# The index keys' projection spread over the opening's four chunks of features, with one transfer per chunk for both weights, in a one-layer decoder kernel

## The chip, the core and the metric

The kernel runs on one core of a Trainium2 chip, as one program. A core has five engines with their own instruction queues: TensorE (PE in the profile) multiplies matrices into PSUM, VectorE (DVE) and ScalarE (ACT) do elementwise work and read PSUM, GpSimd (POOL) does small work and issues some transfers, and SyncE (SP) issues the others. The metric is the device time of one execution in microseconds, here 450.67 (median of three runs, 450.38 to 450.72).

## The reference

One layer of a decoder on 256 tokens of width 1024. The input is normalised, multiplied by one wide matrix, and split into three branches: block-sparse attention A, attention B whose keys are chosen by an indexer, and a recurrent branch C that starts with a causal convolution of `xc`. Cut to what this change is about:

```python
xn = rms_norm(x, g)
proj = xn @ w_in
(qa, ka, va, qb, kb, vb, qi, ki, wi, xc, yc, gates) = jnp.split(proj, IN_OFFSETS, axis=-1)
# indexer of branch B: 8 heads of qi (64 wide), one key ki (64 wide), 8 weights wi per token
dots  = jnp.einsum('bqhd,bsd->bqhs', qiq, ki)
score = jnp.einsum('bqh,bqhs->bqs', wq, jax.nn.relu(dots)) * idx_scale
# causal mask, top 64 keys of each token, attention over them
```

The columns of `w_in` in question: `qi` (512), `ki` and `wi` side by side (64 + 8 = 72, `KW` in the kernel), then `xc` (512) and `yc` (512). After the branches come sigmoid gates, an output projection, an MLP of width 4096 with squared ReLU, and a last normalisation.

## The kernel before, in words

**Precision.** Every f32 operand is split in two parts of a shorter format, `hi` (a copy on ScalarE, L134) and `lo` (the rest, a subtraction on VectorE, L135). A product is three passes: hi x hi, hi x lo, lo x hi (`PASSES`). So each weight tile of 128 x 1024 costs one ScalarE and one VectorE instruction before TensorE can use it, and both engines do this through the whole kernel.

**Weights.** They lie in DRAM as tiles in the order of use. `load` (L137) fetches tile `i` in two halves `raw{i}_0` and `raw{i}_1` of 128 x 1024 through SyncE's queue; five buffers hold raw halves, and a half's buffer is free when its `lo` has been made. `weights()` (L149) hands out the next tile; outside the part written by hand the Tile layer's scheduler places loads, splits and everything else by its own estimate of times.

**The opening** (L327 to L389) is placed by hand: inside `manual_schedule` the engines' instructions stand as written. The 1024 features come in four chunks of 256. For each chunk x (transposed, 256 KB) and a quarter of weight tile 0 (256 KB) are loaded (L232 to L235), ScalarE and VectorE split both, and TensorE makes 12 matmuls of the first half of the index queries, `ps_qi0` (L339 to L345): 2 feature tiles, 2 column tiles, 3 passes. Then follow the second half of the queries, `ps_qi1`, from tile 1; two matmuls that sum the squares of x over features into `ps_r` (L359); and the index keys and weights, `ps_kw`, 24 matmuls from a tile `kw` that is loaded and split as a whole (L238, L360, L376). Its 72 columns are padded with zeros to 128 by GpSimd (L275). In between VectorE computes 1/rms: the variance `v`, a power on GpSimd, one Newton step, `r1`, and two diagonal matrices `dg`, which TensorE multiplies by ones to spread r over all partitions (`rr`, L384). `first_queries(h)` (L284) takes the two halves of the queries out of PSUM. At the end (L386 to L389) the keys are scaled into `ki2`, `pair_keys` (L255) makes `keys2` on ScalarE and `keysl`, `keysh` on VectorE, and `wif` takes the index weights.

**Behind it** the scheduler places the projections `xc` (tiles 2 and 3, accumulators `ps_xc0`, `ps_xc1`), `yc` (tiles 4 and 5), then `vb`, `kb`, `qb` and so on, and puts the index logits (`l0_i0` and the following, L434), which need `keysh`, and the transposes of the index weights (`pt_wi`, L411), which need `wif`, between them. The accumulators share three PSUM buffers (`pacc`, L73): the next one waits until an earlier one has been taken out. `times` (L416) does that on VectorE for `xc`, `yc`, keys and queries. SyncE also reloads x in token order into the buffers of the transposed x (L563), after a small copy on GpSimd that needs `r1`.

Of the kernel before, what the change touches and what calls it, by code (L numbers as in the profile page):

```python
# [28 lines left out]
P = 128  # L29
# [30 lines left out]
def layer(ctx, tc, x, xf, wts, kiwi, small, wri, rel_bias, onehot, gfin, out):  # L60
# [16 lines left out]
    def f(ap):  # L77
        return ap.bitcast(F32)
# [7 lines left out]
    def big(name, dt=F32):  # L86
        return u4.tile([P, 1024], dt, tag="u4", name=name)
# [49 lines left out]
    def load(i):  # L137

        r = []
        for j in range(2):  # L140
            raw = wp.tile([P, 1024], F32, tag="raw", name=f"raw{i}_{j}", bufs=RAW_BUFS)
            nc.sync.dma_start(raw, wts[i, :, j * 1024:(j + 1) * 1024])
            r.append((raw, *(wp.tile([P, 1024], F32R, tag=p, name=f"{p}{i}_{j}", bufs=HL_BUFS) for p in ("hi", "lo"))))
        return r
# [68 lines left out]
    def tmajor(ps, w, xx, t, k0, nk, first, last):  # L213
# [3 lines left out]
        for n, (a, b) in enumerate(PASSES):  # L217
            for k in range(nk):
# [10 lines left out]
    w0 = [tuple(wp.tile([P, 1024], dt, tag=p, name=f"{p}0_{j}", bufs=n)  # L229
                for p, dt, n in (("raw", F32, RAW_BUFS), ("hi", F32R, HL_BUFS), ("lo", F32R, HL_BUFS)))  # L230
          for j in range(2)]
# [42 lines left out]
    for z in (kwh, kwl):  # L274
        nc.gpsimd.memset(f(z[:, :, KW:]), 0.0)  # L275
# [51 lines left out]
    with tc.manual_schedule(engines=ENGINES):  # L327
        pv = ps_q[0].rearrange("p (c t) -> p c t", c=2)
        for i in range(4):
            xi = xr[i // 2].rearrange("p (k t) -> p k t", k=4)  # L330
            d = slice(i % 2 * 512, (i % 2 + 1) * 512)
            raw, hi, lo = (z[:, d] for z in w0[i // 2])
# [6 lines left out]
            for n, (a, b) in enumerate(((0, 0), (0, 1), (1, 0))):  # L339
                for k in (2 * i, 2 * i + 1):  # L340
                    ww = w0[i // 2][1 + a].rearrange("p (k c) -> p k c", k=4)
# [18 lines left out]
        split(kwh[:, :, :KW], kwl[:, :, :KW], kw.rearrange("p (k c) -> p k c", c=KW))  # L360
        write_rows()

# [3 lines left out]
        first_queries(0)  # L366
# [22 lines left out]
        nc.vector.tensor_copy(wif[64:], ps_kw[64:, :S])  # L389
# [20 lines left out]
    for t in range(2):  # L410
        nc.tensor.transpose(pt[:, t * 64:(t + 1) * 64], wif[64:, t * P:(t + 1) * P], ident[64:, 64:])  # L411
    for t in range(2):
        nc.vector.tensor_scalar(wi[:, t, :], pt[:, t * 64:t * 64 + 8], r1[t], r1[t], op0=ALU.mult, op1=ALU.mult)
# [480 lines left out]
def _weight_tiles(w_in, w_pa, w_pb, w_pc, w_o, w_up, w_down):  # L894
# [14 lines left out]
    tiles.append(_fm(w_in[:, 3072:3328])), fm(w_in[:, 3328:3584])  # L909
# [20 lines left out]
    return np.ascontiguousarray(np.stack(tiles))  # L930

# [57 lines left out]
```

## Time and profile before

| | |
|---|---|
| Median of three runs | 450.67 us (450.38 to 450.72) |
| The profiled execution | 450.61 us, of which the traced span 448.8 us |
| TensorE busy | 440.0 us, 98% of the span, 2482 matmuls |
| VectorE busy | 349.6 us, 78% |
| ScalarE busy | 267.7 us, 60% |
| GpSimd busy | 24.1 us, 5% |
| Chain that ended last | TensorE 88%, transfers 4%, GpSimd 3%, VectorE 2% |
| Granted clock of TensorE | 0.999 of full speed on the mean |

How to read it: the page's first part gives busy time by engine, the fourth the chain of work that ended last. The list of waits says who stood still for whom. A timeline lists the instructions of an engine in order of time, equal ones that follow each other merged into one row with a count; the start is where the first of them starts, the duration of such a row reaches to the end of the last. Starts of successive rows give the pitch, which is what a queue of work costs; busy times of matmuls overlap. The names of tiles have their numbers left out in the trace: `ps_xc` is `ps_xc0` or `ps_xc1`, `lo<-raw,hi` any weight split.

### The profile page before, as it was taken

The numbers are of one execution on the slowest core, as the hardware profiler recorded it, in microseconds if no ns is written. First come the engines' busy times: TensorE is split into PE (matmuls) and PEld (weight loads), VectorE is DVE, ScalarE is ACT, GpSimd is POOL, SyncE is SP. The second block draws the span as 40 slices with busy tenths as digits, with TensorE's granted clock in tenths as the row PEclk, the third lists the DMA queues.
The fourth block names the chain that finished last, engine by engine and source line by source line (L and its number), as shares of the span: only waits on it lengthen the run. The fifth ranks groups of instructions, "written<-read, shape, count | busy, mean of one in ns | idle before, by whom it ended". The sixth has DMA issues, their size and how long they took to land.

```text
span 448.8 us, 6931 instructions
## 1 busy us (share of the span) xinstructions
PE 440.0 (98%) x2482; PEld 384.8 (86%) x2482; DVE 349.6 (78%) x687; ACT 267.7 (60%) x459; POOL 24.1 (5%) x61
## 2 busy tenths in 40 slices
PE   7999999999999999999999999999999999999994
PEld 7999899989988888888888888888888888888884
DVE  6799999999999999985888587666666666666646
ACT  6848496964467888675644466544444444444453
POOL 4820100000010100000000000000000000000000
PEclk9999999999999999999999999999999999999999
DMA  7998767436764462565555645465665566565202
GB/s 243 371 271 289 251 177 235 144 101 211 236 192 155 140 211 84 192 198 162 188 185 188 229 153 182 149 198 188 195 191 194 191 189 195 187 203 184 85 0 93
DMA packets 23838, 83.39 MB, mean 186 GB/s; under 512 B 2987, under 2 KB 3020, under 8 KB 23804
## 3 DMA queue, kind: packets, MB, share of 16 engines
q1 hardware_dynamic: 22608, 80.00, 54.6%
q0 software_dynamic: 960, 2.88, 2.3%
q8 instruction: 19, 0.31, 0.3%
q14 instruction: 15, 0.12, 0.1%
q10 hardware_dynamic: 236, 0.08, 0.1%
HBM read 81.11 MB, written 1.83 MB: 185 GB/s over the span
## 4 chain that ended last, share of the span: by engine, by line
PE 88%; DMA 4%; POOL 3%; DVE 2%; ACT 1%; issue 1%; SPq 0%; ACTq 0%; DVEq 0%; POOLq 0%
PE pd L815 19%; PE ps_g L219 15%; PE ps_up L209 13%; PE ps_p L219 7%; PE ps_up L211 7%; PE po L219 5%; DMA raw<-wts 3%; PE ps_qa L199 3%; PE ps_qb L199 3%; PE ps_kb L199 3%; PE ps_ka L199 3%; PE ps_va L219 2%; PE ps_vb L219 2%; DVE lo L135 1%; DMA x<-xf 1%
## 5 line engine op out<-in xcount | busy, mean ns | idle before, releaser
L135 DVE TENSOR_TENSOR lo<-raw,hi 128x1024 fp32r<-128x1024 f32 (+1 forms) x146 | 174.5, 1207 | 59.1 <-ACT hi L134 58.6
L134 ACT ACTIVATE hi<-raw 128x1024 fp32r<-128x1024 f32 (+1 forms) x146 | 149.8, 1045 | 93.1 <-issue 19.6
L209 PE MATMUL ps_up<-x,hi 128*128 128x512 f32 x256 | 64.7, 393 | 0.2 <-DVE x L186 0.2
L209 PEld LDWEIGHTS ps_up<-x,hi 128*128 128x128 f32 x256 | 46.7, 188 | 9.3 <-DVE x L186 0.4
L219 PE MATMUL ps_g<-hi,xn 128*128 128x512 f32 x192 | 53.7, 392 | 0.0
L815 PE MATMUL pd<-hi,hl 128*128 128x512 f32 (+1 forms) x128 | 49.5, 387 | 0.0
L815 PE MATMUL pd<-lo,hh 128*128 128x512 f32 (+1 forms) x128 | 49.4, 386 | 0.0
L815 PE MATMUL pd<-hi,hh 128*128 128x512 f32 (+1 forms) x128 | 49.1, 387 | 0.0
L219 PEld LDWEIGHTS ps_g<-hi,xn 128*128 128x128 f32 x192 | 35.6, 188 | 6.8
L211 PEld LDWEIGHTS ps_up<-x,lo 128*128 128x128 f32 x256 | 35.3, 190 | 2.7
L211 PE MATMUL ps_up<-x,lo 128*128 128x256 f32 x256 | 36.2, 282 | 0.0
L219 PE MATMUL ps_g<-lo,xn 128*128 128x512 f32 x96 | 30.2, 392 | 0.0
L815 PEld LDWEIGHTS pd<-lo,hh 128*128 128x128 f32 x128 | 24.0, 188 | 5.0
L815 PEld LDWEIGHTS pd<-hi,hh 128*128 128x128 f32 x128 | 24.0, 188 | 4.5
L815 PEld LDWEIGHTS pd<-hi,hl 128*128 128x128 f32 x128 | 24.1, 188 | 4.4
L802 ACT ACTIVATE hh<-z 128x512 fp32r<-128x512 f32 x16 | 10.1, 631 | 29.1 <-DVE z L800 29.1
L219 PEld LDWEIGHTS ps_g<-lo,xn 128*128 128x128 f32 x96 | 17.9, 188 | 3.6
L803 DVE TENSOR_TENSOR hl<-z,hh 128x512 fp32r<-128x512 f32 x16 | 11.1, 691 | 9.8 <-ACT hh L802 9.8
L168 POOL TENSOR_TENSOR ssq_n<-q_n 128x1 f32<-128x1 f32 x2 | 0.4, 192 | 277.6 <-ACT scr_n L166 277.6
L796 DVE TENSOR_TENSOR z<-ps_up,u 128x256 f32<-128x256 f32 x32 | 13.4, 418 | 0.0
L684 ACT ACTIVATE g<-ps_g,rh 128x512 f32<-128x512 f32 x12 | 8.2, 684 | 7.0 <-PE ps_g L219 7.0
L795 ACT ACTIVATE u<-ps_up 128x256 f32<-128x256 f32 x32 | 11.8, 368 | 0.0
(344 smaller groups left out, 777.1 us busy)
## 6 DMA issues: line engine op xcount, KB each, us to landing
raw<-wts SPq DMA_DIRECT2D x142, 512.0 KB, 4.8
x<-xf SPq DMA_DIRECT2D x4, 256.0 KB, 4.7
raw<-wts SPq DMA_DIRECT2D x4, 256.0 KB, 4.5
x<-x SPq DMA_DIRECT2D x2, 512.0 KB, 5.0
biasb<-toep POOLq DMA_DIRECT2D x8, 128.0 KB, 6.5
biasa<-toep POOLq DMA_DIRECT2D x8, 128.0 KB, 2.7
out<-o SPq DMA_DIRECT2D x2, 512.0 KB, 2.6
toep<-rrow POOLq DMA_DIRECT2D x1, 766.0 KB, 6.5
```

Of the source, the lines that this page charges most:

```text
L134: nc.scalar.activation(hi, raw, AF.Copy)
L135: nc.vector.tensor_sub(lo, raw, f(hi))
L199: nc.tensor.matmul(pv[:, c, :], ww[a][:, k, :], xx[b][:, k, :], start=(n == 0 and k == 0 and (c == 0 or not part)), stop=(n == 2 and k == ...
L209: nc.tensor.matmul(ps, wh[:, k, :], x2[:, k], start=(k == 0), stop=False)
L211: nc.tensor.matmul(ps[:, :S], wl[:, k, :], x2[:, k, 0], start=False, stop=(k == 7))
L219: nc.tensor.matmul(ps, xx[b][:, k0 + k, d], ww[a][:, k, :], start=(first and n == 0 and k == 0), stop=(last and n == 2 and k == nk - 1))
L684: nc.scalar.activation(g[:, t, :], ps, AF.Tanh, scale=rh[:, t:t + 1])
L795: nc.scalar.activation(u, ps[:, S:], AF.Copy)
L796: nc.vector.tensor_add(z[:, d], ps[:, :S], u)
L802: nc.scalar.activation(hh, z, AF.Copy)
L803: nc.vector.tensor_sub(hl, z, f(hh))
L815: nc.tensor.matmul(ps, hid[g][b][:, c, d], w_down[g][c][a][:, s], start=(g == (NG - LAG if o else 0) and c == 0 and m == 0), stop=(g == NG ...
```

## The change

Two things are moved. First, the index keys and weights: the kernel gets a new input `head`, four blocks of 128 x 656, in each the quarter of weight tile 0 that belongs to a chunk (512 columns) and the 144 columns of kw that belong to the same features; one transfer per chunk brings both. Each chunk splits its part of kw, and after its 12 matmuls of the queries come 6 of `ps_kw`, with 72 columns of weights loaded instead of 128. The separate load and split of `kw` and the zero padding go; `wif` and its transposes shrink to 8 columns. The four blocks take a raw buffer each; before, tile 0 took two.

Second, at the place where the 24 matmuls of `ps_kw` stood, the first half of `xc` (`cs=(0,)` of `ps_xc0`) now stands in the part placed by hand; `first_queries(0)` and the split of tile 2's first half are placed a few lines earlier. The scheduler places what follows anew.

```diff
+    w0r = [wp.tile([P, 1024], F32, tag="raw", name=f"raw0_{i}", bufs=RAW_BUFS)[:, :512 + 2 * KW] for i in range(4)]
     for i in range(4):
-        s, d = slice(i * 512, (i + 1) * 512), slice(i % 2 * 512, (i % 2 + 1) * 512)
-        nc.sync.dma_start(xr[i // 2][:, d], xf[:, s])
-        nc.sync.dma_start(w0[i // 2][0][:, d], wts[0, :, s])
+        nc.sync.dma_start(xr[i // 2][:, i % 2 * 512:(i % 2 + 1) * 512], xf[:, i * 512:(i + 1) * 512])
+        nc.sync.dma_start(w0r[i], head[i])
     loaded[1] = load(1)
-    kw = big("kw")[:, :8 * KW]
-    nc.sync.dma_start(kw, kiwi)
     loaded[2] = load(2)
...
-    for z in (kwh, kwl):
-        nc.gpsimd.memset(f(z[:, :, KW:]), 0.0)
...
             split(hi, lo, raw)
-            for n, (a, b) in enumerate(((0, 0), (0, 1), (1, 0))):
+            split(*(z[:, 2 * i:2 * i + 2, :KW] for z in (kwh, kwl)), kw)
+            for n, (a, b) in enumerate(PASSES):
...
+            for n, (a, b) in enumerate(PASSES):
+                for k in (2 * i, 2 * i + 1):
+                    nc.tensor.matmul(ps_kw[:KW, :S], (kwh, kwl)[a][:, k, :KW], xn[b][:, k, :],
+                                     start=(i == 0 and n == 0 and k == 0), stop=(i == 3 and n == 2 and k == 7))
...
-        split(kwh[:, :, :KW], kwl[:, :, :KW], kw.rearrange("p (k c) -> p k c", c=KW))
         write_rows()
+        first_queries(0)
 
         v, y, b = (sm.tile([P, 2], F32, name=f"{n}_n1", tag=n) for n in ("v", "y", "b"))
         nc.vector.tensor_scalar(v, ps_r[:, S:S + 2], 1.0 / DM, EPS, op0=ALU.mult, op1=ALU.add)
         nc.gpsimd.tensor_tensor(y, v, mhalf.to_broadcast([P, 2]), op=ALU.pow)
-        first_queries(0)
+        split_tile(2, 0)
...
-        split_tile(2, 0)
-        for n, (a, b) in enumerate(PASSES):
-            for k in range(8):
-                nc.tensor.matmul(ps_kw[:, :S], (kwh, kwl)[a][:, k, :], xn[b][:, k, :], start=(n == 0 and k == 0),
-                                 stop=(n == 2 and k == 7))
+        ps_xc = acc_tile("ps_xc0")
+        fmajor(ps_xc, [z[1:] for z in loaded[2]], xn, cs=(0,))
...
-        nc.vector.tensor_copy(wif[64:], ps_kw[64:, :S])
+        nc.vector.tensor_copy(wif[64:KW], ps_kw[64:KW, :S])
...
+        if h == 0:
+            ps = ps_xc
+            fmajor(ps, weights(), xn, cs=(1,))
...
+def _head(w, kw):
+    return np.stack([np.concatenate([_fm(z[i * 256:(i + 1) * 256]) for z in (w, kw)], axis=1) for i in range(4)])
```

What it does to the order of instructions shows at three places. In these rows a weight half keeps its tile's number: `lo4_1` is the lo part of the second half of tile 4. The last number of a name is only a counter, which differs between the two programs.

TensorE at the end of the opening, before: the second half of the queries, the sums of squares, the 24 matmuls of the keys, then xc.

```order
L199 MATMUL ps_qi1_165<-xn2_122,lo1_1_144 128x256 x8
L359 MATMUL ps_r_183<-ones_155,sqs_182 128x1 x2
L378 MATMUL ps_kw_166<-xn2_122,kwh_170 128x256 x16
L378 MATMUL ps_kw_166<-xn2_122,kwl_171 128x256 x8
L199 MATMUL ps_xc0_596<-xn2_122,hi2_0_149 128x256 x16
```

Here the 24 matmuls stand between the sums of squares and xc.

TensorE at the start of the opening now: the first chunk, and the start of the second.

```order
L340 MATMUL ps_qi0_164<-xn2_122,hi0_0_123 128x256 x8
L340 MATMUL ps_qi0_164<-xn2_122,lo0_0_124 128x256 x4
L345 MATMUL ps_kw_166<-xn2_122,kwh_170 72x256 x4
L345 MATMUL ps_kw_166<-xn2_122,kwl_171 72x256 x2
L340 MATMUL ps_qi0_164<-xn2_122,hi0_0_123 128x256 x8
```

The 24 matmuls of `ps_kw` stand in the chunks, six in each, and at their old place xc follows the sums of squares at once.

VectorE before, from the last split of tile 4's first half to the keys: the scaled keys `ki2`, the eviction of xc0 (`xp<-ps_xc0`), then `lo4_1`, the keys and `wif`.

```order
L135 TENSOR_TENSOR lo4_0_804<-raw4_0_801,hi4_0_803 128x1024
L387 TENSOR_TENSOR ki2_176<-ps_kw_166,rr_174 64x256 x2
L503 TENSOR_TENSOR wrl_591<-wrt_588,wrh_590 128x1024
L419 TENSOR_TENSOR xp_594<-ps_xc0_596,rr_174 128x2x256
L135 TENSOR_TENSOR lo4_1_808<-raw4_1_805,hi4_1_807 128x1024
L259 TENSOR_TENSOR keysl_159<-ki2_176,keys2_157 64x256
L260 CAST keysh_158<-keys2_157 64x128
L259 TENSOR_TENSOR keysl_159<-ki2_176,keys2_157 64x256
L260 CAST keysh_158<-keys2_157 64x128
L389 COPY wif_177<-ps_kw_166 64x256
L135 TENSOR_TENSOR lo5_0_876<-raw5_0_873,hi5_0_875 128x1024
L419 TENSOR_TENSOR xp_594<-ps_xc1_646,rr_174 128x2x256
```

The eviction of xc0 stands ahead of `lo4_1` here, and the keys ahead of `lo5_0`.

VectorE now, at the same place.

```order
L135 TENSOR_TENSOR lo4_0_808<-raw4_0_805,hi4_0_807 128x1024
L501 TENSOR_TENSOR wrl_620<-wrt_617,wrh_619 128x1024
L385 TENSOR_TENSOR ki2_174<-ps_kw_166,rr_172 64x256 x2
L135 TENSOR_TENSOR lo4_1_812<-raw4_1_809,hi4_1_811 128x1024
L417 TENSOR_TENSOR xp_623<-ps_xc0_388,rr_172 128x2x256
L135 TENSOR_TENSOR lo5_0_880<-raw5_0_877,hi5_0_879 128x1024
L417 TENSOR_TENSOR xp_623<-ps_xc1_650,rr_172 128x2x256
L256 TENSOR_TENSOR keysl_159<-ki2_174,keys2_157 64x256
L257 CAST keysh_158<-keys2_157 64x128
L256 TENSOR_TENSOR keysl_159<-ki2_174,keys2_157 64x256
L257 CAST keysh_158<-keys2_157 64x128
L387 COPY wif_175<-ps_kw_166 8x256
```

The split `lo4_1` stands ahead of the eviction of xc0, and `lo5_0` and the eviction of xc1 ahead of the keys and `wif`.

TensorE before, from the start of yc0 to the transposes of the index weights.

```order
L199 MATMUL ps_yc0_800<-xn2_122,hi4_0_803 128x256 x16
L199 MATMUL ps_yc0_800<-xn2_122,lo4_0_804 128x256 x8
L199 MATMUL ps_yc0_800<-xn2_122,hi4_1_807 128x256 x6
L434 MATMUL l0_i0_418<-keysh_158,qi_167 128x256
L434 MATMUL l0_i0_418<-keysl_159,qi_167 128x256
L434 MATMUL l0_i0_418<-keysh_158,qil_169 128x256
L411 MATMUL pt_wi_413<-ident_99,wif_177 128x64 x2
```

The logits cut into yc0 after 6 matmuls of its second half.

TensorE now, at the same place.

```order
L199 MATMUL ps_yc0_804<-xn2_122,hi4_0_807 128x256 x16
L199 MATMUL ps_yc0_804<-xn2_122,lo4_0_808 128x256 x8
L199 MATMUL ps_yc0_804<-xn2_122,hi4_1_811 128x256 x16
L199 MATMUL ps_yc0_804<-xn2_122,lo4_1_812 128x256 x2
L432 MATMUL l0_i0_447<-keysh_158,qi_167 128x256
L432 MATMUL l0_i0_447<-keysl_159,qi_167 128x256
L432 MATMUL l0_i0_447<-keysh_158,qil_169 128x256
L409 MATMUL pt_wi_442<-ident_99,wif_175 128x8 x2
```

The first index logits come 42 matmuls after the start of yc0, where they came after 30. In both programs the first matmul of yc0 waits for the eviction of xc0, whose buffer it takes.

## Rows read from the trace of the kernel before

**Rows 1.** Waits of TensorE, whole span: who waited for whom, us, times, longest.
```profile
PE ps_qi L343 <- ACT hi L134: 1.4, 1, 1.4
...
PE ps_up L209 <- DVE x L186: 0.2, 1, 0.2
```

**Rows 2.** Timeline of TensorE: start, us, what, count, [idle before and who ended it].
```profile
6.05 1.21 PE L343 MATMUL ps_qi<-xn,hi 128*128 128x256 f32 x8 [1.36 <-ACT hi L134]
...
7.82 1.22 PE L343 MATMUL ps_qi<-xn,hi 128*128 128x256 f32 x8
...
13.08 2.18 PE L199 MATMUL ps_qi<-xn,hi 128*128 128x256 f32 x16
...
19.66 0.50 PE L359 MATMUL ps_r<-ones,sqs 128*128 128x1 f32 x4
...
20.03 2.16 PE L378 MATMUL ps_kw<-xn,kwh 128*128 128x256 f32 x16
...
22.98 2.08 PE L199 MATMUL ps_xc<-xn,hi 128*128 128x256 f32 x16
```

**Rows 3.** Timeline of ScalarE, 0 to 30 us.
```profile
5.91 0.19 ACT L481 ACTIVATE sab<-sp 128x4 f32<-128x4 f32 x1
...
8.93 0.63 ACT L134 ACTIVATE hi<-raw 128x512 fp32r<-128x512 f32 x1 [0.32 <-DMA raw<-wts]
```

**Rows 4.** Timeline of VectorE, 20 to 39 us.
```profile
20.20 0.16 DVE L364 TENSOR_SCALAR v_n<-ps_r 128x2 f32<-128x2 f32 x1 [1.39 <-PE ps_r L359]
...
20.28 0.41 DVE L288 TENSOR_TENSOR qil<-ps_qi,qi 128x256 fp32r<-128x256 f32 x1
...
22.25 0.16 DVE L367 TENSOR_TENSOR b_n<-y_n 128x2 f32<-128x2 f32 x1 [0.19 <-POOL y_n L365]
...
23.45 1.21 DVE L135 TENSOR_TENSOR lo<-raw,hi 128x1024 fp32r<-128x1024 f32 x1
...
24.69 0.42 DVE L288 TENSOR_TENSOR qil<-ps_qi,qi 128x256 fp32r<-128x256 f32 x1
...
26.51 2.36 DVE L135 TENSOR_TENSOR lo<-raw,hi 128x1024 fp32r<-128x1024 f32 x2
...
31.30 0.86 DVE L387 TENSOR_TENSOR ki<-ps_kw,rr 64x256 f32<-64x256 f32 x2
...
33.33 0.69 DVE L419 TENSOR_TENSOR xp<-ps_xc,rr 128x512 f32<-128x512 f32 x1
...
33.93 1.22 DVE L135 TENSOR_TENSOR lo<-raw,hi 128x1024 fp32r<-128x1024 f32 x1
...
35.06 0.41 DVE L259 TENSOR_TENSOR keysl<-ki,keys 64x256 fp32r<-64x256 f32 x1
...
36.22 0.43 DVE L389 COPY wif<-ps_kw 64x256 f32<-64x256 f32 x1
...
37.67 1.23 DVE L135 TENSOR_TENSOR lo<-raw,hi 128x1024 fp32r<-128x1024 f32 x1 [1.02 <-ACT hi L134]
...
38.93 0.69 DVE L419 TENSOR_TENSOR xp<-ps_xc,rr 128x512 f32<-128x512 f32 x1
```

**Rows 5.** Timeline of TensorE, 34 to 39 us.
```profile
34.94 2.08 PE L199 MATMUL ps_yc<-xn,hi 128*128 128x256 f32 x16
...
38.54 0.28 PE L434 MATMUL l_i<-keysh,qi 128*128 128x256 f32 x1
...
38.99 0.34 PE L411 MATMUL pt_wi<-ident,wif 64*128 64x64 f32 x2
```

**Rows 6.** Timeline of ScalarE, near 36 us.
```profile
36.58 1.06 ACT L134 ACTIVATE hi<-raw 128x1024 fp32r<-128x1024 f32 x1 [2.13 <-DMA raw<-wts]
```

**Rows 7.** Chain that ended last, 0 to 80 us: start, us, what.
```profile
27.77 8.73 DMA raw<-wts
```

**Rows 8.** Timeline of VectorE, near 55 us.
```profile
54.73 0.69 DVE L419 TENSOR_TENSOR y<-ps_yc,rr 128x512 f32<-128x512 f32 x1
```

**Rows 9.** Timeline of TensorE, near 57 us.
```profile
56.85 1.09 PE L219 MATMUL ps_vb<-hi,xn 128*128 128x512 f32 x4
```

More of the change, by code (lines that the diff above doesn't have):

```diff
@@ L59, in layer @@
 @with_exitstack
-def layer(ctx, tc, x, xf, wts, kiwi, small, wri, rel_bias, onehot, gfin, out):
+def layer(ctx, tc, x, xf, head, wts, small, wri, rel_bias, onehot, gfin, out):
     nc = tc.nc
@@ L141, in load @@
             raw = wp.tile([P, 1024], F32, tag="raw", name=f"raw{i}_{j}", bufs=RAW_BUFS)
-            nc.sync.dma_start(raw, wts[i, :, j * 1024:(j + 1) * 1024])
+            nc.sync.dma_start(raw, wts[i - 1, :, j * 1024:(j + 1) * 1024])
             r.append((raw, *(wp.tile([P, 1024], F32R, tag=p, name=f"{p}{i}_{j}", bufs=HL_BUFS) for p in ("hi", "lo"))))
@@ L228, in layer @@
     xr = xt
-    w0 = [tuple(wp.tile([P, 1024], dt, tag=p, name=f"{p}0_{j}", bufs=n)
-                for p, dt, n in (("raw", F32, RAW_BUFS), ("hi", F32R, HL_BUFS), ("lo", F32R, HL_BUFS)))
+    w0 = [tuple(wp.tile([P, 1024], F32R, tag=p, name=f"{p}0_{j}", bufs=HL_BUFS) for p in ("hi", "lo"))
           for j in range(2)]
+    w0r = [wp.tile([P, 1024], F32, tag="raw", name=f"raw0_{i}", bufs=RAW_BUFS)[:, :512 + 2 * KW] for i in range(4)]
     for i in range(4):
-        s, d = slice(i * 512, (i + 1) * 512), slice(i % 2 * 512, (i % 2 + 1) * 512)
-        nc.sync.dma_start(xr[i // 2][:, d], xf[:, s])
-        nc.sync.dma_start(w0[i // 2][0][:, d], wts[0, :, s])
+        nc.sync.dma_start(xr[i // 2][:, i % 2 * 512:(i % 2 + 1) * 512], xf[:, i * 512:(i + 1) * 512])
+        nc.sync.dma_start(w0r[i], head[i])
     loaded[1] = load(1)
-    kw = big("kw")[:, :8 * KW]
-    nc.sync.dma_start(kw, kiwi)
     loaded[2] = load(2)
@@ L331, in layer @@
             d = slice(i % 2 * 512, (i % 2 + 1) * 512)
-            raw, hi, lo = (z[:, d] for z in w0[i // 2])
+            hi, lo = (z[:, d] for z in w0[i // 2])
+            raw, kw = w0r[i][:, :512], w0r[i][:, 512:].rearrange("p (k c) -> p k c", c=KW)
             for k in (2 * i, 2 * i + 1):
@@ L410, in layer @@
     for t in range(2):
-        nc.tensor.transpose(pt[:, t * 64:(t + 1) * 64], wif[64:, t * P:(t + 1) * P], ident[64:, 64:])
+        nc.tensor.transpose(pt[:, t * 8:(t + 1) * 8], wif[64:KW, t * P:(t + 1) * P], ident[64:KW, 64:KW])
     for t in range(2):
-        nc.vector.tensor_scalar(wi[:, t, :], pt[:, t * 64:t * 64 + 8], r1[t], r1[t], op0=ALU.mult, op1=ALU.mult)
+        nc.vector.tensor_scalar(wi[:, t, :], pt[:, t * 8:(t + 1) * 8], r1[t], r1[t], op0=ALU.mult, op1=ALU.mult)
     def times(dst, ps, row):
@@ L508, in layer @@
     for h in range(2):
-        ps = acc_tile(f"ps_xc{h}")
-        fmajor(ps, weights(), xn)
+        if h == 0:
+            ps = ps_xc
+            fmajor(ps, weights(), xn, cs=(1,))
+        else:
+            ps = acc_tile(f"ps_xc{h}")
+            fmajor(ps, weights(), xn)
         times(xp[:, 2 * h:2 * h + 2, 3:], ps, rr)
@@ L907, in col @@
         return w_in[:, o:o + 512]
-    tiles.append(_fm(w_in[:, 3072:3328])), fm(w_in[:, 3328:3584])
+    fm(w_in[:, 3328:3584])
     fm(col(3656)), fm(col(4168))
@@ L970 @@
         "xf": _fm(i["x"][0].T),
+        "head": _head(w_in[:, 3072:3328], w_in[:, 3584:3656]),
         "wts": _weight_tiles(w_in, i["w_pa"][0], i["w_pb"][0], i["w_pc"][0], i["w_o"][0],
                              i["w_up"][0], i["w_down"][0]),
-        "kiwi": _fm(w_in[:, 3584:3656]),
         "small": small,
```

2 lines of the change are left out of this document (1 added, 1 removed).

## The prediction

> **What bounds the kernel now.** I read the page's busy shares first: TensorE is busy for 98% of the span, so a change gains only where TensorE stands still, or by giving it less to do. The list of waits says where it stands still: by its first and its last row [rows 1] TensorE waits for data once at the start and 0.2 us much later, and nothing else of note. The timeline then shows the start in detail [rows 2]. The opening works through four chunks of features; twelve matmuls of the index queries take from 6.05 to 7.82 us, and all 48 end at 13.08, that is 7.03 us. Further on 30 matmuls of the same shape take from 34.94 to 38.54 [rows 5], 0.12 us each. So 48 cost 5.76 us and 1.27 us of the opening is idle, split over four chunks. That is all there is to win here. ScalarE sets the chunks' pace, and at the third its split of the raw weights waits for their transfer [rows 3].
>
> After 13.08 TensorE is dense to the end, so whatever moves its work at 13 us moves the end by the same, unless a new wait comes in between. Whether one does is read from VectorE, which works almost without a break from 20 us on [rows 4].
>
> **The opening, part by part.** The 24 matmuls of index keys and weights stand now at 20.03 to 22.98 [rows 2], 2.95 us. They move into the chunks, six to each. They stay 24 matmuls of 256 columns, so no work goes away; they fill the idle time. 72 matmuls at 0.12 are 8.64 us. I let the first start 0.1 later, since a small activation (0.19 us, [rows 3]) now stands ahead of the first split, and choose another 0.1 for a late second half of the first chunk. The opening then ends at 6.05 + 0.2 + 8.64 = 14.89.
>
> Can the chunks keep up? They come every 1.77 us now (7.82 - 6.05) and TensorE will need 18 x 0.12 = 2.16 per chunk. The weights of a chunk grow from 512 to 656 columns beside 512 of x, 14% more bytes, so a supply bound by transfers comes every 2.02 us; were all of it bound by the weights' transfer it would be 2.27, which costs 3 x 0.11 = 0.33 us. I take 0 and keep 0.33. The kw splits on ScalarE and VectorE, 144 columns per chunk, fit into the 0.39 us by which the period grows; the two fills of kwh and kwl leave GpSimd, which TensorE waits for nowhere in [rows 1].
>
> From 13.08 to the two sums of squares at 19.66 it is 6.58 us [rows 2], unchanged, so they start at 21.47 and the xc half placed by hand 0.37 later (20.03 - 19.66), at 21.84, against 22.98 now: 1.14 us ahead. From there to yc0, the next accumulator, TensorE has the same 48 + 48 matmuls as now, 34.94 - 22.98 = 11.96 us [rows 2, 5]. Without a wait yc0 would start at 33.80.
>
> **The new wait.** yc0 takes the PSUM buffer of xc0, so it waits until VectorE has scaled xc0 out of it. Now that eviction ends at 33.33 + 0.69 = 34.02 and yc0 starts at 34.94 [rows 4, 5]: 0.92 us to spare. In the new order VectorE has one full weight split more (lo4_1) ahead of this eviction, and its chain hangs on the sums of squares. By the pitches of [rows 4], from the start of those sums (19.66): 0.54 to the variance, 0.08 for it, 1.24 for lo2_0, 1.20 for the Newton steps and the two diagonals (22.25 to 23.45), 1.82 for the second queries (24.69 to 26.51), 4.79 for lo2_1 to lo4_0 (26.51 to 31.30), 2.03 for ki2 and wrl (31.30 to 33.33), 1.13 for lo4_1 (33.93 to 35.06), 0.69 for the eviction: 13.52 us. The first queries, which lie behind the variance now, move ahead of it into idle time (VectorE waits 1.39 us there). So xc0's buffer is free at 21.47 + 13.52 = 34.99. TensorE arrives at 33.80 and waits 1.19 us; yc0 starts 0.05 later than now, and the gain is gone. As both paths hang on the sums of squares, an opening that is 0.1 faster or slower moves this sum by 0.1 and no more. With 0.3 us of error in the chain the result here lies between -0.25 and +0.35.
>
> That wait exists because VectorE doesn't look past the split. The row shows the habit: at 37.67 VectorE starts a split after waiting 1.02 us for ScalarE, and the eviction of xc1 at 38.93 stands behind it, though TensorE had finished xc1 before yc0 began at 34.94 [rows 4, 5]. The Trainium skill says it as a rule (PSUM — Partial Sum Buffer, "Engine vs sequencer instructions"): the queues of ScalarE, VectorE and GpSimd are strictly first in, first out. It speaks against this change, and the trace agrees; were evictions able to pass, the sum would be 1.13 us lower.
>
> **The keys behind it.** After yc0 starts, 42 matmuls follow (24 of its first half, 18 of its second) before the first index logits, 5.04 us: TensorE is there at 40.03. These need keysh, and 0.45 us later (38.54 to 38.99, [rows 5]) the transposes need wif. Both now come behind lo5_0 and xc1's eviction on VectorE, and lo5_0 waits for hi5_0, which waits for its transfer. Now ScalarE gets it at 36.58 [rows 6], after a transfer that is issued when lo2_1 is done and takes 8.73 us [rows 7]. In the new order lo2_1 starts at 21.47 + 0.54 + 0.08 + 1.24 + 1.20 + 1.82 = 26.35, 0.16 earlier than its 26.51, so with the same transfer lo5_0 starts at 37.67 - 0.16 = 37.51. Then 1.26 to xc1's eviction, 0.60 for that (33.33 to 33.93), 1.16 for the keys (35.06 to 36.22): keysh is ready at 40.53, half a microsecond after TensorE asks; wif 0.43 later, which the 0.45 covers. If the transfer lands 0.5 us sooner this wait is 0. Ahead of it in the queue one weight tile now goes before the two x loads instead of behind them, the same bytes, so the row alone gives no sign; I take the middle, 0.25, and keep 0 and 0.5.
>
> VectorE falls behind by its longer stand at lo5_0: it could start it at 34.90 (0.60 after the eviction of xc0 starts) and does at 37.26 (the middle), 2.36 us instead of 1.02, less the 0.16, so about 1.2 us. Its eviction of yc0 at 54.73 [rows 8] then ends at 54.73 + 0.69 + 1.18 = 56.60, and the V projection that takes the buffer comes at 56.85 + 0.3 [rows 9]. That still fits by half a microsecond.
>
> The transposes of wi shrink from 64 to 8 columns: 0 to 0.34 us of gain, since the two take 0.34 in all [rows 5]; TensorE waits for their input anyway, and I take 0. Everything else is the same work in nearly the same order under a dense TensorE.
>
> **The sum.** +0.05 at yc0 and +0.25 at the keys: +0.3 us on the profiled execution, which took 450.61 in all. That makes 450.9; the median of the runs is 450.67, so the two stand 0.06 apart. A difference within 0.2%, 0.9 us, is what a measurement of this kernel cannot tell from none.
>
> **Rivals.** *The opening's gain is kept.* VectorE would have to reach xc0's eviction 1.13 us sooner than the pitches say, as if lo4_1 were not ahead of it. Then -1.14 + 0.05 gives 449.5. For it: VectorE has 1.39 us of idle time before the variance, which a shorter path to it would use. Against: the split stands there in the order, and each pitch is a row. Chance 0.07.
>
> *Narrow weights are cheaper.* The 24 moved matmuls load 72 columns of weights instead of 128. If their time went with the loaded columns, 2.95 x 56/128 = 1.29 us would go, the sums of squares would come that much sooner and VectorE's chain with them: 449.6. [Rows 2, 5] speak against: the matmuls run at 0.12 us back to back with 128 loaded columns, and what they stream, 256 columns, stays. Chance 0.04. The Trainium skill (TensorE: Matmul & The Clock Gate, "LDWEIGHTS (loading the stationary operand)") does state that a load's time goes with its columns; no run here shows a load of 72.
>
> *The keys come late: slower.* The mechanism is the transfer of raw5_0. It is issued behind two x loads that wait for r1, and the steps from the variance to r1 and the diagonals end about 1 us later than now (21.47 + 0.54 + 0.08 + 1.24 + 1.20 = 24.53 instead of 23.45, [rows 4]), so these loads sit closer ahead of it. If hi5_0 starts 1 us later than the row's 36.58 allows, at 37.42, keysh is ready at 41.53 and TensorE waits 1.5 us: 450.61 + 0.05 + 1.5 = 452.2. From 0.35 us of lateness the total is slower by more than 0.9. For it: the 8.73 us of [rows 7] show a queue that is long already. Against: the tile ahead of it is issued sooner than now. Chance 0.20.
>
> *The forecast,* a gain in the opening that a wait on VectorE takes back, has 0.69, with 450.4 to 451.5 as its own range: its ends are -0.25 and 0 at yc0 and the keys, and +0.35 + 0.5. The range of 449.7 to 451.9 takes in the near part of the others.
>
> **What would show it.** The opening's matmuls end near 14.9 without gaps, and the sums of squares start near 21.5. The timeline of TensorE has a gap of 1 us or more at yc0, ended by VectorE's eviction of xc0, and a smaller one at the first index logits, ended by keysh. VectorE's lo4_1 starts near 33.2, and lo5_0 waits over 1 us for ScalarE. The forecast is wrong if TensorE is dense from 14.9 to 40, or if the sums of squares come at 21 or sooner.

## The result, and the profile after

The changed kernel takes 455.44 us (455.07 to 456.62, 4 runs) where the kernel before took 450.70 beside it (450.38 to 451.49, 4 runs): a ratio of 1.0104, 95% interval 1.0086 to 1.0123. It is 1% slower, far outside the forecast range (449.7 to 451.9). The profiled execution took 455.36 us, its span 453.6 against 448.8.

TensorE's waits say at once that more than the forecast wait is there (who waited for whom, us, times, longest; [rows 1] had 1.4 and 0.2):

```profile
PE ps_qi L340 <- ACT hi L134: 2.2, 1, 2.2
PE ps_yc L199 <- DVE xp L417: 1.7, 1, 1.7
...
PE l_i L432 <- ACT rl L443: 0.8, 1, 0.8
PE l_i L432 <- DVE keysh L257: 0.5, 1, 0.5
...
```

TensorE's timeline puts them in order of time (start, us, what, count, idle before). It answers to [rows 2, 5]:

```profile
7.09 1.55 PE L340 MATMUL ps_qi<-xn,hi 128*128 128x256 f32 x8 [2.20 <-ACT hi L134]
8.45 1.05 PE L340 MATMUL ps_qi<-xn,lo 128*128 128x256 f32 x4
9.30 1.05 PE L345 MATMUL ps_kw<-xn,kwh 128*72 128x256 f32 x4
...
10.58 1.38 PE L340 MATMUL ps_qi<-xn,hi 128*128 128x256 f32 x8
...
16.58 0.64 PE L345 MATMUL ps_kw<-xn,kwh 128*72 128x256 f32 x4
17.06 0.40 PE L345 MATMUL ps_kw<-xn,kwl 128*72 128x256 f32 x2
17.30 2.08 PE L199 MATMUL ps_qi<-xn,hi 128*128 128x256 f32 x16
...
23.78 0.50 PE L360 MATMUL ps_r<-ones,sqs 128*128 128x1 f32 x4
24.14 2.16 PE L199 MATMUL ps_xc<-xn,hi 128*128 128x256 f32 x16
...
38.17 2.15 PE L199 MATMUL ps_yc<-xn,hi 128*128 128x256 f32 x16 [1.73 <-DVE xp L417]
...
43.90 0.39 PE L432 MATMUL l_i<-keysh,qi 128*128 128x256 f32 x1 [0.47 <-DVE keysh L257]
...
48.77 0.39 PE L432 MATMUL l_i<-keysh,qi 128*128 128x256 f32 x1 [0.85 <-ACT rl L443]
```

Read the starts. The first product begins at 7.09, not 6.05. The first chunk's 18 products take until 10.58, 3.49 us where 18 x 0.12 = 2.16 were forecast: four products need 0.85 us (8.45 to 9.30), 0.21 each. The last chunk is at full speed, narrow products too: four in 0.48 us (16.58 to 17.06). TensorE's granted clock says why (stretch, busy times, and as the third column from the end the granted clock, PEclk):

```profile
6.00:8.00 2.00, 0.91 (x6) 0.91 (x7) 1.81 (x5) 2.00 (x8) 0.00 (x0) 0.94 1.03 388
8.00:10.00 2.00, 2.00 (x12) 2.00 (x11) 2.00 (x7) 1.89 (x7) 1.21 (x3) 0.50 0.79 188
10.00:12.00 2.00, 2.00 (x14) 2.00 (x13) 1.36 (x4) 0.63 (x2) 1.74 (x6) 0.71 0.88 300
```

It falls to 0.50, the 1.2 GHz level, after TensorE had stood idle for 2.20 us; whether the idle time is the reason is tested below. ScalarE's timeline shows what the start waited for, and what the keys do later:

```profile
5.52 0.91 ACT L330 ACTIVATE xn<-x,sp 128x256 fp32r<-128x256 f32 x2 [2.85 <-DMA sp<-small]
...
39.87 1.06 ACT L134 ACTIVATE hi<-raw 128x1024 fp32r<-128x1024 f32 x1 [7.24 <-DMA raw<-wts]
40.84 1.71 ACT L255 ACTIVATE keys<-ki 64x256 fp32r<-64x256 f32 x4
...
46.46 1.99 ACT L134 ACTIVATE hi<-raw 128x1024 fp32r<-128x1024 f32 x2
48.35 0.84 ACT L443 ACTIVATE rl<-l_i 128x256 f32<-128x256 f32 x2
```

The table of small parameters, sp, lands 4.8 us after its issue; before it was 3.8. These are the rows of the transfers, after and before (KB, then us from issue to landing):

```profile
sp<-small ACTq DMA_DIRECT2D x1, 24.0 KB, 4.8
```

```profile
sp<-small ACTq DMA_DIRECT2D x1, 24.0 KB, 3.8
```

The split of a late weight tile, hi5_0, starts at 39.87 after ScalarE has waited 7.24 us for its transfer, and the copies of the keys stand behind it. That transfer is issued when lo2_1 is done, as forecast, and takes 9.16 us where [rows 7] had 8.73:

```profile
30.63 9.16 DMA raw<-wts
```

VectorE's chain behind the sums of squares is the forecast one, a little longer ([rows 4]):

```profile
24.32 0.16 DVE L365 TENSOR_SCALAR v_n<-ps_r 128x2 f32<-128x2 f32 x1 [0.40 <-PE ps_r L360]
24.51 1.23 DVE L135 TENSOR_TENSOR lo<-raw,hi 128x1024 fp32r<-128x1024 f32 x1
26.36 0.16 DVE L368 TENSOR_TENSOR b_n<-y_n 128x2 f32<-128x2 f32 x1 [0.62 <-POOL y_n L366]
...
29.38 2.36 DVE L135 TENSOR_TENSOR lo<-raw,hi 128x1024 fp32r<-128x1024 f32 x2
...
31.78 2.35 DVE L135 TENSOR_TENSOR lo<-raw,hi 128x1024 fp32r<-128x1024 f32 x2
34.05 1.22 DVE L501 TENSOR_TENSOR wrl<-wrt,wrh 128x1024 fp32r<-128x1024 f32 x1
35.30 0.87 DVE L385 TENSOR_TENSOR ki<-ps_kw,rr 64x256 f32<-64x256 f32 x2
36.20 1.23 DVE L135 TENSOR_TENSOR lo<-raw,hi 128x1024 fp32r<-128x1024 f32 x1
37.34 0.68 DVE L417 TENSOR_TENSOR xp<-ps_xc,rr 128x512 f32<-128x512 f32 x1
40.97 1.22 DVE L135 TENSOR_TENSOR lo<-raw,hi 128x1024 fp32r<-128x1024 f32 x1 [2.94 <-ACT hi L134]
42.11 0.68 DVE L417 TENSOR_TENSOR xp<-ps_xc,rr 128x512 f32<-128x512 f32 x1
42.71 0.41 DVE L256 TENSOR_TENSOR keysl<-ki,keys 64x256 fp32r<-64x256 f32 x1
```

At 26.36 VectorE waits for GpSimd's power. GpSimd's rows for it, after and before:

```profile
24.57 1.76 POOL L366 TENSOR_TENSOR y_n<-v_n,mhalf 128x2 f32<-128x2 f32 x1 [1.93 <-DVE v_n L365]
```

```profile
21.35 0.86 POOL L365 TENSOR_TENSOR y_n<-v_n,mhalf 128x2 f32<-128x2 f32 x1
```

Term by term:

| term | forecast | trace after |
|---|---|---|
| first product | 6.15 | 7.09 |
| opening, 72 products | 8.64 (and 0.1) | 10.21 (7.09 to 17.30) |
| sums of squares at | 21.47 | 23.78 |
| from there to the end of xc0's eviction | 13.52 | 14.24 (to 38.02) |
| wait at yc0 | 1.19 | 1.73 |
| wait at the first index logits | 0.25 | 0.47 |
| wait at the second | 0 | 0.85 |
| yc0 starts at, against 34.94 before | 34.99 | 38.17 |

So 3.23 us are lost by yc0, and 0.47 + 0.85 more at the logits: 4.55 of the span's 4.8.

### The profile page after: what moved, and what is told of

Same layout as the page of the kernel before. It is cut to its first block, busy times and chain, and to the rows that moved or that the text cites. A ratio compares the mean times of both kernels' runs of the same rounds, so it can differ in the third digit from the quotient of the medians.

```text
span 453.6 us, 6933 instructions
## 1 busy us (share of the span) xinstructions
PE 441.2 (97%) x2482; PEld 386.4 (85%) x2482; DVE 349.6 (77%) x690; ACT 267.4 (59%) x462; POOL 24.5 (5%) x59
## 4 chain that ended last, share of the span: by engine, by line
PE 92%; DMA 3%; ACT 3%; DVE 1%; issue 1%; ACTq 0%
PE pd L817 19%; PE ps_g L219 14%; PE ps_up L209 13%; PE ps_p L219 7%; PE ps_up L211 7%; PE po L219 5%; PE ps_qa L199 3%; PE ps_qb L199 3%; PE ps_ka L199 3%; PE ps_kb L199 3%; PE ps_vb L219 2%; PE ps_va L219 2%; DMA raw<-wts 2%; ACT hi L134 2%; PE ps_qi L340 2%; PE ps_qi L199 1%
```

## The experiments

Each ratio is to the kernel before, run beside it on the same chip. "Before" and "changed" in a line say from which kernel it was made.

### The first product's late start

**blocks_alone.** Changed, with the 24 products and the first xc group put back where the kernel before has them; only the loads and the splits by chunk stay.

> The changed loads alone: the four blocks of 656 columns and the splits of the keys' columns with their chunk, but the 24 products of the keys stand where the kernel before has them and the first group of xc is the scheduler's again. Theory D (the bigger blocks make the small table and the first chunk of x land later): the small table lands 4.8 us after its issue instead of 3.8, the first product starts at 7.1 instead of 6.05, and with 9 warming products the granted clock falls as well; time 452.0 to 453.0. Rival E (the late landing has to do with the rest of the change or is chance of one execution): first product near 6.05, clock 1.00, 450.4 to 451.0.

Measured: 452.57 us, ratio 1.0045 (1.0032 to 1.0057). sp lands after 4.6 us, first product at 6.90, granted clock 0.56 from 8 to 10 us. The loads alone cost 2.0 us by the ratio, before a single product has moved.

**rows_768, rows_apart, two_transfers.** Changed, with the rows padded, spaced, or fetched in two parts:

```
-  w0r = [wp.tile(...)[:, :512 + 2 * KW] for i in range(4)]
+  w0r = [wp.tile(...)[:, :768] for i in range(4)]       # rows_768; head padded with zeros
...
-  nc.sync.dma_start(w0r[i], head[i])
+  nc.sync.dma_start(w0r[i], head[:, i*656:(i+1)*656])  # rows_apart: blocks side by side
+  nc.sync.dma_start(w0r[i][:, :512], head[i, :, :512])   # two_transfers
+  nc.sync.dma_start(w0r[i][:, 512:], head[i, :, 512:])   # two_transfers
```

> The changed kernel with each block's rows filled with zeros from 656 to 768 columns (2,624 to 3,072 bytes), so the opening loads 0.23 MB more. Theory F (bytes on the queue ahead make the small table late): it lands later than 4.8 us after its issue, by as much again for 112 columns as for 144, so near 5.5; first product near 7.7, time 456 to 457. Rival G (the odd length of a row makes packets slow): it lands 3.8 us after its issue, first product near 6.1, clock 1.00, time near 453.5.

> The changed kernel with the four blocks laid side by side in memory, so that the rows of one block are 10,496 bytes apart, as the rows of a weight tile and of x are 8,192 bytes apart in the kernel before, and not end to end. Same bytes, same issues, same order on every engine. Theory K (rows that follow one another in memory make the first transfers slow): the small table lands 3.8 to 4.0 us after its issue, first product near 6.1, clock 1.00, time near 453.5. Rival L (it is the longer rows, 2,624 bytes against 2,048, in line with the other transfers): it lands 4.4 to 4.9 us after its issue, as in the changed kernel, time 455.4.

> The changed kernel with each block loaded in two transfers, 512 columns (2,048 bytes a row, as in the kernel before) and 144 columns (576 bytes a row), from and to the same places; 9 warming products; the scheduler's order behind the opening differs somewhat. Read for the landing of the small table alone. Theory N (what makes the first transfers land late is rows of 2,624 bytes in the queue beside them): it lands 3.8 us after its issue, first product near 6.1. Theory O (it is the bytes that the keys' columns put between the first chunks, in whatever rows): 4.4 to 4.9 us, first product near 7. Time 454 to 456 in both, since the sixth transfer on the loading queue still waits for the table and is now the keys' part of the second chunk.

Measured: 454.34 (1.0051 to 1.0099), 455.25 (1.0070 to 1.0112) and 453.10 us (1.0040 to 1.0080); sp lands after 4.9, 4.6 and 4.7 us. Neither the length nor the spacing of the rows does it, and 112 columns more make it 0.1 later, not 0.7. Theory O alone fitted all three, until the next runs. (In the first and the last of the three the scheduler put the keys elsewhere, and no logits wait.)

**before_own_array, blocks_in_weights, blocks_last.** Before, with its opening tile from an array of its own; changed, with the blocks moved into the big weight array; changed, with the array of blocks declared last.

```
-  nc.sync.dma_start(w0[i // 2][0][:, d], wts[0, :, s])
+  nc.sync.dma_start(w0[i // 2][0][:, d], head[i])              # before_own_array
-  nc.sync.dma_start(w0r[i], head[i])
+  nc.sync.dma_start(w0r[i], wts[i // 3, :, i % 3 * 656:i % 3 * 656 + 656])  # blocks_in_weights
```

> The kernel before with its opening tile read from an array of its own, four blocks of 512 columns with no keys' columns; same bytes, transfers and order on every engine as before. Theory P (reading the first chunks from a separate array makes the first transfers land late): the small table lands 4.4 to 4.9 us after its issue instead of 3.8, the first product starts at 6.8 to 7.1, time 450.9 to 451.6 (the opening's gaps take none of it). Theory Q (the keys' bytes do it): 3.7 to 4.0 us, first product near 6.05, time 450.5.

> The changed kernel with its four blocks of 656 columns laid into two tiles at the front of the big weight array, rows 8,192 bytes apart as in the kernel before, and the separate array gone; same bytes, transfers and order on every engine as in the changed kernel. Theory P: the small table lands 3.7 to 4.0 us after its issue, first product near 6.1; with 9 warming products the clock is as likely full as not, time 453.5 to 454.5. Theory Q: it lands 4.4 to 4.9 us after its issue, first product near 7, time 455.4.

> The changed kernel with the array of blocks declared as the last of its inputs instead of the third, so that it and the others may lie elsewhere in memory; nothing else differs. Theory R (it is where the inputs lie in memory): the small table lands 3.7 to 4.0 us after its issue, first product near 6.1, time near 454. If the array's place does not matter: 4.4 to 4.9 us and 455.4.

The first row is ScalarE's of before_own_array, the second that of blocks_in_weights:

```profile
5.36 0.91 ACT L334 ACTIVATE xn<-x,sp 128x256 fp32r<-128x256 f32 x2 [2.68 <-DMA sp<-small]
```

```profile
4.47 0.91 ACT L330 ACTIVATE xn<-x,sp 128x256 fp32r<-128x256 f32 x2 [1.78 <-DMA sp<-small]
```

Measured: 451.10 us (1.0008 to 1.0032), 455.17 (1.0057 to 1.0116) and 454.79 (1.0076 to 1.0106). Without one byte of the keys the separate array delays the start by 0.8 us; with all of the keys' bytes, from the big array, the start is as early as before. Theory P, and O falls: two_transfers was late for its array. Over all profiles sp lands 3.7 to 4.0 us after its issue where the opening comes from the big array (8 profiles) and 4.4 to 4.9 where it comes from its own (10). Its place among the inputs does not matter; why a separate array is slower stays open. One rival is left: the rows of the big array lie 8,192 bytes apart, and no run laid them so in an array of their own (the spacings tried there are 2,048, 2,624, 3,072 and 10,496 bytes). blocks_in_weights got little of its early start into the time: its opening ran at half clock from the first product, and its keys waited 1.40 us.

### The clock in the first chunk

**warm11.** Changed, `WARM = 9` to 11: two more products of zeros before the first useful one. Every engine keeps its order.

> The changed kernel with 11 instead of 9 warming products; every engine keeps its order of instructions. Two of them are 0.84 us, so TensorE's idle time before its first useful product shrinks from 2.20 to 1.36 us, which is what the kernel before had. Theory A (the granted clock fell because TensorE had stood idle longer): the granted clock stays at 1.00 from 6 to 12 us, the first chunk of 18 products takes about 2.2 us instead of 3.49 and the second 2.16 instead of 2.41, and the sums of squares come 1.5 us earlier (near 22.2); VectorE's work behind them follows, so the time falls by 1.0 to 1.6 us, to about 454.1. Rival B (the clock fell for what runs in the opening itself, the keys' products among the others): the granted clock falls as before and the time stays at 455.4. Rival C (the clock recovers, but the keys still wait for the weight tile that lands at 39.8 us): sums of squares 1.5 us earlier, first index logits still near 43.9, time above 454.9.

```profile
8.00:10.00 2.00, 2.00 (x19) 2.00 (x18) 1.88 (x6) 2.00 (x7) 1.34 (x4) 1.00 1.00 251
```

```profile
PE ps_yc L199 <- DVE xp L417: 1.7, 1, 1.7
PE l_i L432 <- DVE keysh L257: 1.3, 1, 1.3
```

Measured: 454.28 us, ratio 1.0083 (1.0069 to 1.0098; the interval overlaps the changed kernel's). In the profile the numbers of theory A and of rival C both come out: clock 1.00, sums of squares at 21.93, 1.85 earlier (0.35 of it the start), and the keys take 0.83 back, waiting 1.30 instead of 0.47. The wait at yc0 stays at 1.73 to the hundredth, since VectorE's chain moves along with the sums.

**before_warm7, before_warm6, before_warm11.** Before, with 7, 6 and 11 warming products.

> The kernel before with 7 instead of 9 warming products; every engine keeps its order. TensorE's idle time before its first useful product grows from 1.36 to about 2.2 us, as in the changed kernel. Theory A: the granted clock falls in the opening here too (to 0.5 in some 2 us); the 48 products of the opening have 1.27 us of gaps that take up a part, so the opening ends 0.3 to 1.6 us later and the time is 451.0 to 452.3. Rival B (the fall needs the changed opening): clock 1.00 throughout, 450.7 as before.

> The kernel before with 6 warming products; every engine keeps its order. With 7, TensorE stood idle for 1.76 us and the clock stayed; with the blocks alone it stood idle for 1.77 us, later, and the clock fell. Theory A (idle time alone decides): at about 2.2 us of idle, as much as in the changed kernel, the granted clock falls to 0.5 here as well, and the time rises to 451 to 452. Rival B (the fall needs more than idle time): clock 1.00, 450.4.

> The kernel before with 11 warming products; every engine keeps its order. Its opening waits for its chunks (1.27 us of gaps in the profiled execution), and with 6 and 7 warming products these gaps took up nearly all of the time at half clock (0.0 and 0.3 us slower). So more warming should give nothing either: 450.2 to 450.6. If the changed kernel's gain from two more warming products (1.1 us) were something other than the clock, it would show here as well: 449.3.

Measured: 450.55 us (0.9992 to 1.0009), 450.77 (0.9998 to 1.0016) and 450.12 (0.9978 to 0.9996). I had read the first of them wrongly when I wrote the second's expectation: the granted clock's column stays at 1.00, but the products do not keep full speed. In before_warm6 (TensorE's timeline, then the stretch):

```profile
5.99 2.08 PE L343 MATMUL ps_qi<-xn,hi 128*128 128x256 f32 x8 [1.98 <-ACT hi L134]
7.86 1.05 PE L343 MATMUL ps_qi<-xn,lo 128*128 128x256 f32 x4
```

```profile
6.00:8.00 2.00, 2.00 (x9) 2.00 (x10) 1.88 (x5) 1.96 (x6) 0.68 (x2) 1.00 0.96 315
```

Eight products in 1.87 us are 0.23 each: half speed. Yet the sums of squares come at 20.20, only 0.54 after [rows 2]. The opening before waits for its chunks anyway, and its 1.27 us of idle time take most of the slow products in. The changed opening has no idle time left, so it pays in full. With 11, the kernel before gains 0.13%, and its 12 runs lie within 0.5 us where 29 of the kernel before beside them spread over 2.2: that the two products take the spread away by way of this clock is likely, but no run shows it execution by execution.

Where the profile shows half speed varies from one profile to the next: with 9 warming products it is there from the first product in rows_apart, one_piece and blocks_in_weights, from about 8 us in the changed kernel, blocks_alone and rows_768, and not at all in before, two_transfers, before_own_array and blocks_last. So theory A's reason, the longer idle time, does not hold by itself: half speed follows 0.65 us of idle time in one_piece and 0.76 in blocks_in_weights, full speed 1.55 to 1.62 in the last three named. With 11 the opening is at full speed in all six profiles, but for the first eight products of three_out (1.21 us). The Trainium skill (TensorE: Matmul & The Clock Gate, "What's actually happening") says that the chip's watch on activity runs free of the kernel, so that the same kernel warms at another point each time. These profiles fit that; as they are of different kernels, they do not test it.

### VectorE's queue and the keys

**wrl_on_pool.** Changed with 11 warming products, and the low part of the gate weights on GpSimd.

```
-    nc.vector.tensor_sub(wrs[1], wrt, f(wrs[0]))
+    nc.gpsimd.tensor_sub(wrs[1], wrt, f(wrs[0]))
```

> The changed kernel with 11 warming products, and with the low parts of the gate weights (one subtraction of 128x1024, 1.04 us on VectorE, which stands between the splits of the weight tiles and the eviction of the first xc group) on GpSimd, which is idle there. Everything else up to the first yc group keeps its order, but behind it the scheduler now puts the keys' copies on ScalarE ahead of the split of the late weight tile, and the keys on VectorE ahead of its low part. Theory H (TensorE's 1.73 us before the first yc group are VectorE's queue behind the sums of squares): the wait falls by 1.0, to about 0.7 us. Theory I (the 1.30 us before the first index logits are the keys' place behind a late weight tile): that wait goes. Both: 454.3 - 1.0 - 1.3 = 452.0, and 451.2 if the 0.8 us at the second index logits go as well. Rival J (these waits hide others that come as late): 454.0 or more.

Measured: 454.55 us (1.0073 to 1.0100). The time is rival J's. The logits' waits went, as theory I has it, but yc0 waited 2.77 where theory H had 0.7. Rows of VectorE, GpSimd and TensorE:

```profile
30.03 4.74 DVE L135 TENSOR_TENSOR lo<-raw,hi 128x1024 fp32r<-128x1024 f32 x2
```

```profile
30.14 2.41 POOL L501 TENSOR_TENSOR wrl<-wrt,wrh 128x1024 fp32r<-128x1024 f32 x1
```

```profile
37.67 2.56 PE L199 MATMUL ps_yc<-xn,hi 128*128 128x256 f32 x16 [2.77 <-DVE xp L417]
40.03 1.91 PE L199 MATMUL ps_yc<-xn,lo 128*128 128x256 f32 x8
```

The same two splits took 2.35 us in the changed kernel; here they take 4.74, longer by 2.39, and GpSimd's subtraction beside them takes 2.41. VectorE lost more than it was spared, TensorE stood idle for 2.77 us, and eight products then took 1.71 us (40.03 to 41.74), half speed again.

**wrl_behind.** Instead the split of the gate weights is made to wait for the eviction; GpSimd does only the column. The lines shown are a part of the edit, which also moves them behind the loop with the eviction.

```
+    nc.gpsimd.tensor_scalar(one, xp[:, 0, S+2:S+3], 0.0, 1.0, op0=ALU.mult, op1=ALU.add)
-    nc.scalar.activation(wrs[0], wrt, AF.Copy)
+    nc.scalar.activation(wrs[0], wrt, AF.Copy, scale=one)
```

> The changed kernel with 11 warming products, and with the split of the gate weights (1.05 us on ScalarE, 1.04 us on VectorE) made to wait for the first xc group's eviction, by a factor of 1 that is computed from a column of it. The keys' copies stand ahead of the late weight tile's split again, as when the subtraction was on GpSimd, but GpSimd now does nothing beside VectorE. Theory H: VectorE's queue from the sums of squares to that eviction is shorter by 1.04 us, so TensorE's wait before the first yc group falls from 1.73 to about 0.7 us. Theory I: with the keys ahead of the late tile the 1.30 and 0.8 us at the index logits go. Both: 454.3 - 3.1 = 451.2; H alone 453.3, I alone 452.2. Rival J (what waits there only hides later waits, or the gate weights come too late for their products at 56 us): 453.5 or more.

```profile
PE l_i L432 <- ACT rl L443: 0.6, 1, 0.6
PE ps_yc L199 <- DVE xp L417: 0.6, 1, 0.6
```

```profile
32.88 1.73 ACT L255 ACTIVATE keys<-ki 64x256 fp32r<-64x256 f32 x4 [2.12 <-DVE ki L385]
38.17 1.06 ACT L134 ACTIVATE hi<-raw 128x1024 fp32r<-128x1024 f32 x1 [3.56 <-DMA raw<-wts]
```

Measured: 451.75 us, ratio 1.0030 (1.0015 to 1.0045), against 1.0083 for warm11: half a per cent for the place of one split and of what the scheduler moves with it. The wait at yc0 falls by 1.13 to 0.60, and with the keys ahead of the late tile the first logits do not wait at all. Theory H holds, and theory I for the first logits; the second still wait 0.62 us, where both were to go.

### Versions that might have won

**one_piece, one_piece_late_wrl.** No blocks: the opening tile as before, the keys' weights in one transfer behind its second piece, their products behind chunks 2, 3 and 4. The first has 9 warming products and wrl on GpSimd, the second 11 and wrl behind the eviction.

> A version without the blocks: the opening weight tile in four pieces of 512 columns as in the kernel before, the keys' weights in one transfer of 288 KB behind the second piece; the keys' 24 products stand behind the second (12), third (6) and fourth (6) chunk of the opening; 9 warming products; half of xc by hand and the gate weights' low part on GpSimd. If the blocks made the start late and nothing else: small table 3.8 us after its issue, first product near 6.05, clock 1.00, opening of 72 products ends near 15.0 to 15.5, sums of squares near 21.7; VectorE's queue behind them, 13.2 us, gives the first yc group at 35.0 to 35.5 with a wait near 0.7, and 450.0 to 450.9, level with the kernel before. If the late landing has another cause: first product near 7, 451.5 or more.

> The version without blocks (keys' weights in one transfer behind the second piece of the opening tile), with 11 warming products and the gate weights' split behind the first xc eviction. With the start near 6.1 and full clock the opening's 72 products end near 15.0, the sums of squares come near 21.5 against 22.54 for the kernel before with its 24 keys' products counted in (19.66 + 2.88), and the wait before the first yc group is near 0.7: 450.4 - 1.0 + 0.7 = 450.1, between level and 0.3 us faster than the kernel before. If the opening runs at half clock again, as it did with 9 warming products: 451.5 to 452.

Measured: 453.81 us (1.0060 to 1.0085) and 451.19 (1.0004 to 1.0027). Both miss their expectations, 450.0 to 450.9 and 450.1. Both start early (5.93 and 6.05). The first then ran its first 20 products at half speed and had VectorE beside GpSimd. The second has its sums of squares at 21.81, 0.73 ahead of the kernel before with the keys counted in (22.54), and gives 0.59 back at yc0 and 0.36 at the second logits.

**three_out.** Changed, blocks kept, all three causes out: blocks in the big array, 11 warming products, wrl behind the eviction.

> The changed kernel, its blocks kept, with all three causes taken out: blocks read from the front of the big weight array, 11 warming products, the gate weights' split behind the first xc eviction. Same order on every engine as in the run with the last two alone (451.75). Ledger theory: the start is 0.8 us earlier (6.05 against 6.85) and nothing behind it takes that back, since the keys no longer stand behind the late tile: 450.9, within 0.2% of the kernel before. Rival S (a fourth cause): the wait before the first yc group or at the index logits grows by what the start gains: 451.7.

```profile
PE l_i L432 <- ACT rl L443: 0.8, 1, 0.8
PE ps_yc L199 <- DVE xp L417: 0.6, 1, 0.6
```

Measured: 451.72 us (1.0024 to 1.0058), rival S's 451.7 and not 450.9; not told apart from wrl_behind. In its profile the 11 warming products lasted until 6.1, so the first product came at 6.32, 0.5 earlier instead of 0.8, and the second logits waited 0.76 instead of 0.62. yc0 stands at 34.90, where the kernel before has it (34.94): the wait of 0.60 there takes the interleaving's gain back to the last tenth. The 0.76 behind it is about what the profiled span lies above that of the kernel before (449.5 against 448.8). The medians lie 1.3 us apart; the profile does not show the rest of that.

The fastest kernel of all is before_warm11: 0.13% ahead of the kernel before, less than the 0.2% that count as a difference here.

## Why the prediction was wrong

- **The start ("I let the first start 0.1 later"): the first step that failed.** It came 1.04 later. I priced the change of the loads by bytes and by the activation ahead of the split, and did not ask when the first transfers land. The separate array makes the first product 0.8 late; in the kernel before it costs 0.5 us by itself in the medians, 0.9 by the ratio (before_own_array).
- **72 products at 0.12: right in number, wrong in speed; the second step.** Nothing in [rows 2] showed a product at half speed, so I had no term for it. The cover was there to be seen: 1.27 us of idle time, which I counted as pure gain. Filling it took away what hid a slow clock: 1.57 us in the profile. Two more warming products gave back 1.2 us in the medians, though the intervals of the two ratios overlap.
- **Chunks keep up: right here.** From the second chunk on TensorE is dense, and the last two take 2.15 us each. It is not sure at full speed: in blocks_last, with the same loads, TensorE waited 0.47 us for the last chunk; warm11 had no such gap.
- **Narrow products cost as much: right;** that rival is dead (four in 0.48 us).
- **The wait at yc0: right in place, cause and order, 1.73 for 1.19.** The chain from the sums was 14.24 for 13.52; 0.62 of the difference is VectorE's wait for GpSimd's power, which the sum let lo2_0 cover. The power took 1.76 us beside that split, 0.86 before; whether the split held it up is not tested. TensorE in turn arrived 0.33 later than forecast and started 0.15 after the eviction's end. That the wait hangs on VectorE's order, wrl_behind shows.
- **The keys: the third step that failed.** The 0.47 at the first logits lies within 0 to 0.5, but by luck: TensorE and keysh both came 3.4 late (43.43 for 40.03, 43.90 for 40.53). The chance of 0.20 for late keys named the tile raw5_0, and it is the one: hi5_0 was to start at 36.42 and started at 39.87. At the second logits I had no wait, since I followed the keys only through VectorE. They stand behind hi5_0 on ScalarE as well, and the activation of the first logits, which frees the buffer of the second, stands there behind two more weight splits (46.46 to 48.45): 0.85. Whatever the opening gains, the keys can give back. In the changed kernel, warm11, blocks_in_weights, blocks_last and rows_apart the first logits wait for keysh, 0.47 to 2.31 us, and in all five the span ends 409.6 to 409.7 us after they start. The tile's transfer took 9.16, 9.99, 10.10, 9.70 and 11.01 us there, against 8.73 before; why it varies stays open.
- **The sum.** The first logits came 3.62 us after the forecast's 40.28 (40.03 and the middle, 0.25), and the second waited 0.85: 4.47, the whole miss (455.36 against 450.9). On the way to the first logits 0.94 came from the start, 1.47 from the slow opening (10.21 less the 8.74 forecast), 0.72 from the sums of squares to lo2_1, 0.42 from there to hi5_0; 0.25 is my choice of the middle, and 0.18 was made up. These are not prices that can be saved one by one. warm11 had its sums of squares 0.46 behind the forecast and still took 454.37 in the profile, 3.5 above it. wrl_behind had them 0.58 behind, and with the gate weights' split and the keys in other places it took 451.57, 0.7 above. So in these runs most of the miss hangs on what stands where in the queues of VectorE and ScalarE behind the opening.

## What to carry to other kernels

A block of weights moved into an array of its own is a change of the loads even if no byte is added: look at the landing of the first transfers, and try the same rows inside the old array. Idle time of TensorE in a stretch that waits for data may be hiding a slow clock; before filling it, see whether products there always run at full speed, and in more than one execution. Where a stretch of dense work is moved forward, follow its consumers through every queue they stand in, not only the one that the trace names.

## What the runs showed of the hardware

- The small table, one of the first transfers, lands 0.4 to 1.2 us later in the kernels that read the opening weights from a separate input array (4.4 to 4.9 us against 3.7 to 4.0), with rows of 2,048 to 3,072 bytes and the array third or last among the inputs. Open: why, and whether rows 8,192 bytes apart would be late too.
- The granted clock's column can show 1.00 over a stretch whose products take 0.23 us instead of 0.12; products are the safer clock. The Trainium skill (TensorE: Matmul & The Clock Gate, "Seeing it yourself") warns that the trace's clock events have been seen to be unreliable, and this case agrees.
- A subtraction with two SBUF inputs on GpSimd held VectorE up for its whole length: 2.39 us lost beside 2.41 us of work. The Trainium skill (SBUF — State Buffer, "SBUF: two separate sides") states an exclusive lock on the ports that the two share, held for the whole instruction. The numbers agree.
